# A two-layer streaming encoder on one core: attention cut into stages, a new order at the head, casts and rates moved

## The chip, the cores and the metric

The kernel runs on one core of one Trainium2 chip. A core has TensorE (PE: matrix products into the accumulators' memory, PSUM), VectorE (DVE), ScalarE (ACT), GpSimd (POOL) and SyncE (SP), which work through their own instructions in order and wait for one another through semaphores. DMA transfers are issued from the queues of SP, ACT or POOL. The metric is the device time of one execution in microseconds (us), as the median of several runs.

## The reference

x is 256 tokens by 2048 channels, c one conditioning row. Two layers, all in fp32:

```python
for l in range(DEPTH):
    mod = (c_act @ w_mod[l] + b_mod[l]).reshape(bn, 6, d)
    shift_m, scale_m, gate_m, shift_f, scale_f, gate_f = ...
    h = layer_norm(x) * (1.0 + scale_m) + shift_m
    proj = h @ w_in[l]
    uv, q_c, kv_c, k_r, sb, sc, sh, ag = jnp.split(proj, IN_SPLITS, axis=-1)
    y_a = gmlp_mixer(uv, ...)                 # chunked spatial gating
    y_b = mla_mixer(q_c, kv_c, k_r, ...)      # latent attention, 4 heads
    y_c = short_conv_mixer(sb, sc, sh, ...)   # width 3
    y_d = conformer_conv(ag, ...)             # GLU, width 31, norm, swish
    y = jnp.concatenate([y_a, y_b, y_c, y_d], axis=-1) @ w_out[l]
    x = layer_norm(ALPHA * x + (1.0 + gate_m) * y, ...)
    h = layer_norm(x) * (1.0 + scale_f) + shift_f
    y = conv_ffn(h, ...)                      # 2048 -> 2 x 5632 -> 2048
    x = layer_norm(ALPHA * x + (1.0 + gate_f) * y, ...)
```

The attention normalises q_c and kv_c by their root mean square, makes queries, keys and values from them, rotates a part of the queries and one shared key, and takes a softmax over the keys of the same or earlier 64-token chunks.

## The kernel before

**Weights.** Every weight is read once, in tiles of 1 MB (`raw_tile`, four buffers) or 512 KB. Most are split into two halves of a rounded type, so that a product costs three fast passes: ScalarE casts the high half (`whi`, line 397), DVE subtracts for the low half (`wlo`, line 398). Some tiles are used "exact" (`wexact`, line 381), as plain fp32 without a split; a plain product is issued as two records of TensorE.

**Modulation.** `w_mod` is multiplied by c on DVE, in passes over 1 MB tiles: `row_sum` (line 192) for shifts and scales, `mod_step` (line 227) for gates. A generator, `mod_stream`, deals these passes out. `stream` (line 339) calls `pump` once for each unit of products, and `RATES` (line 35) says how many passes a unit of each stage takes along.

**Scheduling.** The code gives the order of the program. A scheduler then sets the order on each engine: earlier code has precedence, and later instructions that are ready go ahead where an earlier one waits. `tc.add_manual_dep` adds a dependency by hand, one kind for order on the same engine alone, the other with a semaphore.

**Head.** SP's queue begins with the identity matrix (`cst`), the columns of c (`ccol`), x and the first mod weights. ScalarE applies Silu to c; products with a matrix of ones spread it over the partitions (`cB`). `normed_T` takes the statistics of x for two tiles of 128 tokens, each with its own root (`power`, on POOL); ScalarE normalises a quarter, TensorE transposes it, and ScalarE copies it to `hF`.

**Layer 0's mixers**, `by_pieces`, go through the 16 blocks (kt) of 128 channels of h as they come: for each, two mod passes, one `mod_done` (line 205), then the scale and shift on `hF` (line 1455). From block `PLAIN_KT` = 4 on, `hF` is split into `hT` by `split` (line 415: the cast on ScalarE, line 417, the subtraction on DVE, line 418). `turns` lists the order of products: groups D, U, V, B and E, with D's accumulators in PSUM throughout and the others' sums held outside, brought in (line 1224) and put back (line 1229) by ScalarE. The copy that puts back is ordered behind the casts of the D tile, if that is the very next turn. Then B's remaining units run, and `mix_b` at their end; then C's units (`mix_ce`), then the output projection.

**Attention**, `mix_b` (line 958), loads its weights (into three raw buffers in layer 1), reads B's accumulators out (squares, scaled copies), and goes straight on: sums of squares (`ps_ss`), roots, rotated key (`ps_kr`), queries (`ps_qn`, `ps_qr`), keys (`ps_kn`), values (`ps_v`), scores and softmax for three groups (`ps_sc`), transposes (`ps_pT`) and the weighted values (`ps_o`). All of this comes in the program ahead of the first products of group C.

PSUM has six banks for accumulators and two for short-lived tiles (`ms_tile`). `load_params` loads the small parameters of a layer on POOL's queue. Both kinds of background work, the taps of the 31-wide convolution (`prodD` on ScalarE, `convD` on DVE in layer 0), are dealt out by `STEPS`.

## Time and profile before

| What | Value |
|---|---|
| median of 3 runs | 2246.07 us (2244.87 to 2246.17) |
| the profiled execution | 2246.46 us |
| its span, first to last instruction | 2244.7 us |
| mean granted TensorE clock | 0.991 |
| HBM read | 601.05 MB |

The profile gives the busy time of each engine, in total and by windows of time, with the clock granted to TensorE and the share of time in which the 16 DMA engines worked. In a timeline each row is a run of like instructions: start, length, engine, line, operation, tile written <- tiles read, count; in brackets the idle time of the engine ahead of it and what ended it. Records of TensorE overlap slightly.

### The profile page before, as it was taken

Reading aid. Unit: us, or ns where it says so; the run is one execution under the profiler, and the core shown is the slowest. Engines: PE = TensorE matmul, PEld = TensorE weight load, DVE = VectorE, ACT = ScalarE, POOL = GpSimd, SP = SyncE. Lnnn points to the kernel's source line nnn. Section 1 sums busy time; section 2 is a strip of 40 time slices with the busy share of each in tenths; the row PEclk is TensorE's granted clock in tenths of the full one; section 3 lists DMA queues with packets and bytes.
Section 4 is the critical chain, followed back from the end, with each engine's and each line's share of the span. In section 5 each row is a group of like instructions: output and inputs, shape, how many; then the busy total and the mean of one; then the engine's idle time right before and its main releaser. Section 6 shows DMA issues by size and latency. Waiting matters only on the chain.

```text
span 2244.7 us, 30821 instructions
## 1 busy us (share of the span) xinstructions
PE 2200.6 (98%) x12128; PEld 1901.5 (85%) x12128; DVE 1738.9 (77%) x2222; ACT 1067.3 (48%) x1579; POOL 29.6 (1%) x49
## 2 busy tenths in 40 slices
PE   7999999999999999999999999999999999999997
PEld 5788885898888888888889899888888888888886
DVE  6778986988888888989876998977775656575756
ACT  3457541454455445544444435445444544454542
POOL 0000000000000000000000000000000000000000
PEclk9999999999999999999999999999999999999999
DMA  9999689688888888888867666865665555555553
GB/s 390 350 390 386 239 340 359 247 308 315 313 316 308 329 318 320 328 330 322 336 219 263 209 232 252 305 224 208 245 224 192 184 199 179 203 189 188 187 194 144
DMA packets 94235, 605.17 MB, mean 270 GB/s; under 512 B 10660, under 2 KB 10852, under 8 KB 28932
## 3 DMA queue, kind: packets, MB, share of 16 engines
q1 hardware_dynamic: 93752, 602.29, 71.8%
q8 instruction: 95, 1.56, 0.3%
q0 software_dynamic: 336, 0.89, 0.1%
q14 instruction: 52, 0.43, 0.1%
HBM read 601.05 MB, written 2.10 MB: 269 GB/s over the span
## 4 chain that ended last, share of the span: by engine, by line
PE 80%; DVE 4%; DMA 1%; ACT 1%; issue 1%; POOL 0%; DVEq 0%; ACTq 0%; POOLq 0%
PE g_c L94 23%; PE v_c L94 22%; PE d L94 21%; PE o L94 5%; PE C_c L94 2%; PE D_c L94 2%; PE U_c L94 1%; PE B_c L94 1%; PE E_c L94 1%; DVE wlo L398 1%; DMA wraw<-in_w_out_dram 1%; DVE convD L827 1%; PE ps_xT L534 0%; DVE wmod L192 0%; DMA wmod<-in_w_mod_turned_dram 0%
## 5 line engine op out<-in xcount | busy, mean ns | idle before, releaser
L397 ACT CAST whi<-wraw 128x1024 fp32r<-128x1024 f32 (+1 forms) x632 | 647.9, 1045 | 873.2 <-PE g_c L94 208.1
L398 DVE TENSOR_TENSOR wlo<-wraw,whi 128x1024 fp32r<-128x1024 f32 (+1 forms) x632 | 752.9, 1214 | 307.6 <-ACT whi L397 290.0
L94 PE MATMUL d<-whi,a 128*128 128x512 f32 x1344 | 364.1, 389 | 0.0
L94 PE MATMUL v_c<-hT,whi 128*128 128x512 f32 (+1 forms) x1456 | 341.8, 383 | 0.0
L94 PE MATMUL g_c<-hT,whi 128*128 128x512 f32 (+1 forms) x1344 | 313.3, 380 | 0.0
L192 DVE SCALAR_TENSOR_TENSOR wmod<-wmod,cB 128x2048 f32<-128x2048 f32 x126 | 287.4, 2286 | 31.9 <-DMA wmod<-in_w_mod_turned_dram 31.6
L94 PEld LDWEIGHTS v_c<-hT,whi 128*128 128x128 f32 x1456 | 264.5, 189 | 48.2 <-DVE g L1388 0.3
L94 PEld LDWEIGHTS d<-whi,a 128*128 128x128 f32 x1344 | 252.2, 188 | 52.5 <-ACT whi L397 0.2
L94 PEld LDWEIGHTS g_c<-hT,whi 128*128 128x128 f32 x1344 | 243.4, 189 | 43.2
L94 PE MATMUL d<-wlo,a 128*128 128x512 f32 x672 | 209.9, 389 | 0.0
L94 PE MATMUL v_c<-hT,wlo 128*128 128x256 f32 x1400 | 190.2, 283 | 0.0
L94 PEld LDWEIGHTS v_c<-hT,wlo 128*128 128x128 f32 x1400 | 183.1, 191 | 6.5
L94 PE MATMUL g_c<-hT,wlo 128*128 128x256 f32 x1280 | 175.8, 283 | 0.0
L94 PEld LDWEIGHTS g_c<-hT,wlo 128*128 128x128 f32 x1280 | 168.2, 191 | 5.9
L227 DVE SCALAR_TENSOR_TENSOR macc<-wmod,cact,macc 128x2048 f32<-128x2048 f32 x60 | 140.7, 2345 | 17.3 <-DMA wmod<-in_w_mod_gates_dram 17.2
L94 PEld LDWEIGHTS d<-wlo,a 128*128 128x128 f32 x672 | 126.2, 188 | 26.2
L94 PE MATMUL o<-whi,a 128*128 128x512 f32 x384 | 109.7, 395 | 2.4 <-ACT whi L397 2.4
L94 PEld LDWEIGHTS o<-whi,a 128*128 128x128 f32 x384 | 71.8, 188 | 20.1 <-ACT whi L397 4.1
L94 PE MATMUL D_c<-hT,whi 128*128 128x256 f32 x432 | 81.6, 292 | 1.7 <-ACT whi L397 1.7
L1337 DVE SCALAR_TENSOR_TENSOR u<-g,pf,u 128x254 f32<-128x254 f32 (+1 forms) x176 | 73.3, 476 | 0.0
L94 PEld LDWEIGHTS D_c<-hT,whi 128*128 128x128 f32 x432 | 68.8, 197 | 4.4 <-ACT whi L397 2.8
L94 PE MATMUL o<-wlo,a 128*128 128x512 f32 x192 | 63.0, 397 | 0.6 <-DVE wlo L398 0.5
(343 smaller groups left out, 2505.4 us busy)
## 6 DMA issues: line engine op xcount, KB each, us to landing
wraw<-in_ffn_w_up_dram SPq DMA_DIRECT2D x168, 1024.0 KB, 4.9
wmod<-in_w_mod_turned_dram SPq DMA_DIRECT2D x126, 1024.0 KB, 6.3
wraw<-in_ffn_w_down_dram SPq DMA_DIRECT2D x88, 1024.0 KB, 4.8
wmod<-in_w_mod_gates_dram SPq DMA_DIRECT2D x64, 1024.0 KB, 5.0
wraw<-in_w_in_dram SPq DMA_DIRECT2D x27, 1024.0 KB, 5.5
wraw<-in_w_out_dram SPq DMA_DIRECT2D x26, 1024.0 KB, 5.8
wexact<-in_w_in_dram SPq DMA_DIRECT2D x46, 512.0 KB, 9.6
wexact<-in_ffn_w_up_dram SPq DMA_DIRECT2D x16, 512.0 KB, 9.5
```

Of the source, the lines that this page charges most:

```text
L94: pe.matmul(o, lhsT, rhs, start=start, stop=stop, skip_group_check=True)
L192: i = dve.scalar_tensor_tensor(out=raw, in0=raw, scalar=1.0, in1=cB[:, k0 : k0 + n], op0=ALU.mult, op1=ALU.mult, accum_out=total)
L227: i = dve.scalar_tensor_tensor(out=acc, in0=w, scalar=col, in1=acc, op0=ALU.mult, op1=ALU.add)
L397: cast[0] = act.copy(hi[:, :m], r)
L398: i = dve.tensor_tensor(out=lo[:, :m], in0=r, in1=hi[:, :m].bitcast(F32), op=ALU.subtract)
L827: dve.scalar_tensor_tensor(out=yd[:, j, 30 - k :], in0=glu[:, j, : S - 30 + k], scalar=CW(k, j), in1=yd[:, j, 30 - k :], op0=ALU.mult, op1 ...
L1337: dve.scalar_tensor_tensor(out=u[:, sh:], in0=x[:, : S - sh], scalar=col(k, j), in1=u[:, sh:], op0=ALU.mult, op1=ALU.add)
```

## The change

- **Head.** `ccol` and `cst` are loaded from ScalarE's queue, so x is first on SP's. The matrix of ones is a DVE memset. The two variances are put side by side, and one root serves both tiles. The first `row_sum` waits for that root.
- **Idle products.** `warm` multiplies the ones with some tile into a PSUM tile that nothing reads: once on a constant at the start, once on each token tile's first normalised quarter, and once on the first mod weights.
- **Casts.** The high half of `hT` is copied by DVE. The list of casts ahead of which a sum may not be put back holds the cast of D's weights alone, and reaches over the next two turns.
- **Rates.** Layer 0: group C 1.5 to 2.0, output projection 1.53 to 1.17.
- **Attention.** What follows the read-out of B's accumulators is cut into seven steps. `stream` runs one of them behind the products of each of C's units, from the first unit on. The operations are the same.
- **Parameters.** Layer 1's are loaded behind layer 0's last parameter load.

```diff
-    dict(B=1.3, C=1.5, out=1.53, first=1.2, up=0.68, down=0.7),
+    dict(B=1.3, C=2.0, out=1.17, first=1.2, up=0.68, down=0.7),
...
+    ccol = keep.tile([P, 16], F32, name="ccol")
+    act.dma_start(out=ccol, in_=A["c_cols"])
     cst = keep.tile([P, 1024], F32, name="cst")
-    nc.sync.dma_start(out=cst[:, 0:128], in_=consts[:, 0:128])
+    act.dma_start(out=cst[:, 0:128], in_=consts[:, 0:128])
+    cact = keep.tile([P, 16], F32, name="cact")
+    act.activation(out=cact, in_=ccol, func=AF.Silu)
...
+    flat = slot("flat")[:, :512]
+    pool.memset(flat, 1.0)
+    onesR = keep.tile([P, P], F32R, name="onesR")
+    dve.memset(onesR.bitcast(F32), 1.0)
+    ones = onesR.bitcast(F32)
...
+    def warm(x, n):
+        ps = ms_tile("warm")
+        for _ in range(n):
+            mm(ps[:, : x.shape[1]], ones, x, True, True)
+
+    warm(flat, 1)
...
-        row_sum(raw, D, 0, total)
+        i = row_sum(raw, D, 0, total)
+        if root:
+            tc.add_manual_dep(i.ins, root.pop().ins.name, data_dep, reason="the root is not to wait for this pass")
+            warm(raw[:, 0:512], 1)
...
         item = load()
+        begun = bool(staged)
         flush()
+        if begun:
+            staged.pop(0)()
         pending.append(lambda: products(item))
...
+            steps = (
+                (sums,),
+                (queries, keys_scaled),
+                (keys,),
+                (lambda: scores(0, 0), lambda: scores(1, 0)),
+                (lambda: turned(0, 0), lambda: turned(1, 0), lambda: scores(1, 1)),
+                (lambda: turned(1, 1),),
+                (values,),
+            )
+            staged.extend(lambda fs=fs: [f() for f in fs] for fs in steps)
...
-                    casts[k].append(cast[0])
+                    casts[k] = cast[0]
...
-                g1, k1 = turns[n + 1] if n + 1 < len(turns) else ("", ())
-                side(g, kts, casts.get(k1[0], ()) if g1 == "D" else ())
+                side(g, kts, [casts[k[0]] for h, k in turns[n + 1 : n + 3] if h == "D" and k[0] in casts])
...
-            power(r[:, 0:1], r[:, 0:1])
             scale.append(r)
+        rs = smallp.tile([P, 2], F32, tag="rsin", name="rs_in")
+        root[:] = [power(rs, var)]
...
+            if q == 0:
+                warm(xn, 1)
...
             if kt >= PLAIN_KT:
-                casts[kt] = [split([h[:, kt % 2, :] for h in hT[kt // 2][:2]], x)]
+                hi, lo = (h[:, kt % 2, :] for h in hT[kt // 2][:2])
+                dve.tensor_copy(hi, x)
+                dve.tensor_tensor(out=lo, in0=x, in1=hi.bitcast(F32), op=ALU.subtract)
...
-            load_params(l + 1)
+            load_params(l + 1, params[0])
```

More of the change, by code (lines that the diff above doesn't have):

```diff
@@ L110, in encoder_kernel @@
     sinT = cst[:, 768:1024]
-    flat = tmp_tile("flat")
-    pool.memset(flat[:, 0:P], 1.0)
-    pool.memset(flat[:, P : P + 16], 0.0)
-    for j in range(4):
-        pool.memset(flat[:, P + 5 * j : P + 5 * j + 1], 1.0)
-    onesR = keep.tile([P, P + 16], F32R, name="onesR")
-    act.copy(onesR, flat[:, : P + 16])
-    ones = onesR[:, 0:P].bitcast(F32)
+    flat = slot("flat")[:, :512]
[3 more added lines that the diff above has]
+    ones = onesR.bitcast(F32)
     mhalf = keep.tile([P, 4], F32, name="mhalf")
@@ L124, in power @@
     def power(o, i):
-        pool.tensor_tensor(out=o, in0=i, in1=mhalf[:, : i.shape[1]], op=ALU.pow)
+        return pool.tensor_tensor(out=o, in0=i, in1=mhalf[:, : i.shape[1]], op=ALU.pow)
     X = []
@@ L131, in encoder_kernel @@
         X.append(x_t)
-    ccol = keep.tile([P, 16], F32, name="ccol")
-    nc.sync.dma_start(out=ccol, in_=A["c_cols"])
-    cact = keep.tile([P, 16], F32, name="cact")
-    act.activation(out=cact, in_=ccol, func=AF.Silu)
     W = {
@@ L195, in row_sum @@
         held(i, "mod")
+        return i
+    root = []
     def mod_unit(l, m, kt, total):
@@ L1067, in mix_b, with sums @@
-            for blk in range(2):
+            v = {}
+            def sums():
+                ps = ms_tile("ps_ss")
+                for t in range(2):
+                    for j in range(3):
+                        mm(ps[:, t : t + 1], sqs[j][:, t * P : (t + 1) * P], ones[:, 0:1], j == 0, j == 2)
+                    for j in range(2):
+                        mm(ps[:, 2 + t : 3 + t], sqs[3 + j][:, t * P : (t + 1) * P], ones[:, 0:1], j == 0, j == 1)
+                v["rr"] = rr = smallp.tile([P, 8], F32, tag="rr", name="rr")
+                dve.tensor_scalar(
+                    out=rr[:, 0:2], in0=ps[:, 0:2], scalar1=1.0 / Q_LORA, scalar2=RMS_EPS, op0=ALU.mult, op1=ALU.add
+                )
+                dve.tensor_scalar(
+                    out=rr[:, 2:4], in0=ps[:, 2:4], scalar1=1.0 / KV_LORA, scalar2=RMS_EPS, op0=ALU.mult, op1=ALU.add
+                )
+                power(rr[:, 4:8], rr[:, 0:4])
+                dve.tensor_scalar(out=rr[:, 4:6], in0=rr[:, 4:6], scalar1=ATT_SCALE, scalar2=None, op0=ALU.mult)
+                v["dg"] = dg = tmp_tile("dgB")
+                for t in range(2):
+                    dve.tensor_scalar(
+                        out=dg[:, t * P : (t + 1) * P], in0=ident, scalar1=rr[:, 6 + t : 7 + t], scalar2=None, op0=ALU.mult
+                    )
+                v["rope"] = rope = slot("rope").rearrange("p (j s) -> p j s", j=4)
+                ps = ms_tile("ps_kr")
+                mm(ps[:, :S], idup, kc[0:64, 0:S], True, False)
+                mm(ps[:, :S], rotdup, kc[0:64, S : 2 * S], False, True)
+                pool.memset(rope[64:128, 2, :], 0.0)
+                pool.memset(rope[0:64, 3, :], 0.0)
+                act.copy(rope[0:64, 2, :], ps[0:64, :S])
+                act.copy(rope[64:128, 3, :], ps[64:128, :S])
@@ L1119, in mix_b @@
[L1119 to L1127 removed]
+                v[(blk, g)] = pt
@@ new lines, in turned @@
+            def turned(blk, g):
+                pt = v[(blk, g)]
+                if blk == 0:
+                    v["pT0"] = slot("pT0").rearrange("p (h s) -> p h s", h=4)
+                    v["pT1"] = slot("pT1")[:, :512].rearrange("p (h s) -> p h s", h=4)
+                pT0, pT1 = v["pT0"], v["pT1"]
+                ps = ms_tile("ps_pT")
+                for i in range(4):
+                    pe.transpose(ps[:, i * P : (i + 1) * P], pt[:, i * P : (i + 1) * P], ident)
+                if blk == 0:
+                    dve.tensor_copy(pT0[:, :, 0:P], ps.rearrange("p (h s) -> p h s", h=4))
+                else:
+                    p4 = ps.rearrange("p (h k s) -> p h k s", h=2, k=2)
+                    dve.tensor_copy(pT0[:, 2 * g : 2 * g + 2, P : 2 * P], p4[:, :, 0, :])
+                    dve.tensor_copy(pT1[:, 2 * g : 2 * g + 2, :], p4[:, :, 1, :])
@@ new lines, in values @@
+            def values():
+                vv, pT0, pT1 = v["vv"], v["pT0"], v["pT1"]
+                Y["b"] = slot("yb").rearrange("p (j s) -> p j s", j=4)
+                for b in range(2):
+                    ps = ms_tile("ps_o")
+                    for hh in range(2):
+                        h = 2 * b + hh
+                        o = ps[:, hh * S : (hh + 1) * S]
+                        mm(o, vv[:, 0, h * P : (h + 1) * P], pT0[:, h, :], True, False)
+                        mm(o[:, P : 2 * P], vv[:, 1, h * P : (h + 1) * P], pT1[:, h, :], False, True)
+                    act.copy(Y["b"][:, 2 * b : 2 * b + 2, :], ps.rearrange("p (j s) -> p j s", j=2))
@@ L1408, in normed_T @@
         scale = []
+        var = smallp.tile([P, 2], F32, tag="vin", name="v_in")
         for t in range(2):
```

226 lines of the change are left out of this document (94 added, 132 removed).

## Prediction, written before the result was known

> **What bounds the kernel now.** I read the page first, for the engines' shares, then the busy time by windows, to find where TensorE is idle or its clock is down, and last the waits and timelines of those places.
>
> ```profile
> PE 2200.6 (98%) x12128; PEld 1901.5 (85%) x12128; DVE 1738.9 (77%) x2222; ACT 1067.3 (48%) x1579; POOL 29.6 (1%) x49
> ```
>
> TensorE is busy for all but 2244.7 - 2200.6 = 44.1 us of the span, and half of that lies ahead of its first real product. The change adds products and takes none away, so it can win only idle time and time at a lowered clock.
>
> ```profile
> core 0: us, PE busy (x) PEld busy (x) DVE busy (x) ACT busy (x) POOL busy (x), PEclk, DMA share, GB/s
> 19.90:25.30 5.40, 5.40 (x13) 4.32 (x14) 3.90 (x3) 1.62 (x3) 0.00 (x0) 0.50 1.02 413
> 50.00:58.50 8.50, 8.50 (x39) 6.84 (x39) 1.27 (x4) 2.96 (x6) 0.00 (x0) 1.00 0.84 342
> 58.50:76.80 18.30, 18.06 (x103) 15.12 (x102) 16.03 (x20) 10.01 (x18) 0.00 (x0) 1.00 0.80 309
> 76.80:86.80 10.00, 7.11 (x35) 6.83 (x35) 8.75 (x10) 4.38 (x7) 0.00 (x0) 0.66 0.92 300
> 86.80:208.60 121.80, 119.39 (x656) 101.39 (x654) 100.55 (x109) 67.62 (x128) 4.21 (x8) 1.00 1.00 402
> 208.60:220.00 11.40, 8.84 (x36) 7.77 (x36) 10.24 (x16) 11.25 (x32) 1.02 (x1) 0.70 1.01 413
> 220.00:300.00 80.00, 79.60 (x383) 67.68 (x382) 66.70 (x88) 38.79 (x85) 2.68 (x1) 1.00 0.70 258
> 330.00:347.00 17.00, 14.22 (x57) 9.85 (x56) 14.41 (x15) 5.99 (x6) 0.00 (x0) 1.00 1.00 372
> 1297.40:1325.00 27.60, 27.60 (x160) 23.51 (x160) 25.00 (x55) 8.15 (x15) 1.10 (x1) 1.00 0.53 203
> ```
>
> The losses in reach stand in these rows. At half clock 5.4 us of work cost 2.7 too much (first row). At 76.8 there are 2.9 us idle and 0.34 x 10 = 3.4 lost to the clock; at 208.6, 2.6 idle and 0.30 x 11.4 = 3.4; at 330, 2.8 idle. In layer 1's attention (last row) nothing is idle. But from 86.8 to 208.6 the DMA share is 1.00: there the transfers set the pace, and TensorE can arrive earlier only by as much as they do. They lost 0.16 x 8.5 + 0.20 x 18.3 + 0.08 x 10 = 5.8 us between 50 and 86.8.
>
> **The head.** SyncE issues x third; DVE's first row sum shares its time with the root for tile 1.
>
> ```profile
> 0.74 0.40 SPq L104 DMA_DIRECT2D cst<-in_consts_dram  x1
> 1.19 0.42 SPq L134 DMA_DIRECT2D ccol<-in_c_cols_dram  x1
> 1.66 0.42 SPq L1407 DMA_DIRECT2D x<-in_x_dram  x1
> ```
> ```profile
> 10.99 0.56 POOL L125 TENSOR_TENSOR r_in<-r_in,mhalf 128x1 f32<-128x1 f32 x1 [7.71 <-DVE r_in L1417]
> 13.84 2.59 POOL L125 TENSOR_TENSOR r_in<-r_in,mhalf 128x1 f32<-128x1 f32 x1 [2.29 <-DVE r_in L1417]
> ```
> ```profile
> 13.74 2.28 DVE L192 SCALAR_TENSOR_TENSOR wmod<-wmod,cB 128x2048 f32<-128x2048 f32 x1
> ...
> 18.27 0.16 DVE L205 TENSOR_TENSOR mod<-total,bcol 128x2 f32<-128x2 f32 x1
> 19.43 0.41 DVE L1455 TENSOR_SCALAR hF<-hF,mod 128x256 f32<-128x256 f32 x1 [1.00 <-ACT hF L1430]
> ```
> ```profile
> 5.64 6.64 PE L94 MATMUL ps_c<-diag,onesR 128*128 128x512 f32 x8 [5.64 <-DVE diag L160]
> ```
>
> With the two small loads on ScalarE's queue, x is issued at 0.74 and everything behind it on SyncE moves 0.92 us. ScalarE pays two issues of some 0.4 us ahead of the Silu, which waits for its data anyhow. The shared root starts when tile 1's statistics are there, at 13.84 - 0.92 = 12.9, and takes 0.6 (the lone row) instead of 2.59, since the row sum now waits for it. Queued behind that wait on DVE are both sums and the first mod, all needed by the first product: 13.5 + 2 x 2.28 + 0.16 + 0.41 = 18.6, and with the few hundredths between the rows 18.7. ScalarE's path, which ended last before (the 1.00 us wait in the last DVE row), is then done sooner, at about 17. The first product comes at 18.7 for 19.90: 1.2.
>
> The idle products are four pairs of 512-column records. At ps_c's 6.64 / 8 = 0.83 us they take 6.6 at half clock, 3.3 at full. Three pairs stand between the root and 18.7, in time that TensorE has idle, so I cost them at nothing; were the last one late, it would cost up to 1.7. The pair that reads the first mod weights holds their raw buffer by as much, and SyncE's next load waits for it, beside a DMA that is full (1.02). If they hold the clock up, the 2.7 goes; I take 2.0, as the switch comes at an instant that no row fixes. Head: 1.2 + 2.0 = 3.2, between 0.9 (the issue alone) and 3.9.
>
> **The order of the casts.** This is the largest term (layer 0's D group, with the others' turns between its tiles).
>
> ```profile
> 54.99 0.58 ACT L1229 COPY sumU<-U 128x512 f32<-128x512 f32 x1 [6.99 <-PE U L94]
> ...
> 58.20 0.42 ACT L417 CAST hT<-hF 128x256 fp32r<-128x256 f32 x1
> 58.50 1.05 ACT L397 CAST whi<-wraw 128x1024 fp32r<-128x1024 f32 x1
> ```
> ```profile
> 58.65 0.42 DVE L418 TENSOR_TENSOR hT<-hF,hT 128x256 fp32r<-128x256 f32 x1 [7.23 <-ACT hT L417]
> 59.59 1.23 DVE L398 TENSOR_TENSOR wlo<-wraw,whi 128x1024 fp32r<-128x1024 f32 x1 [0.52 <-ACT whi L397]
> ```
> ```profile
> 50.73 0.33 SPq L386 DMA_DIRECT2D wraw<-in_w_in_dram  x1
> 60.84 0.33 SPq L200 DMA_DIRECT2D wmod<-in_w_mod_turned_dram  x1
> ```
>
> A cast of hT stood on ScalarE behind copies that waited for TensorE's U products; DVE waited 7.23 us for it, its raw buffers stayed full, and SyncE issued nothing from 50.73 to 60.84. The new code makes hT's high half on DVE, and puts the casts of D's weights ahead of the sum copies when D is one or two turns away; U(2,3) was not covered before. DVE then gets past at about 52, wlo at 53.5, and the queue refills some 7 us earlier. The added DVE copies are 12 of 128x256: I take 0.41 (the hF row; not shown itself, between nothing and that), 4.9 us in all, against twelve round trips to ScalarE of about the same length that fall away. A sum copy now waits for a cast, and so for a transfer; behind it TensorE's next bank waits, but D's products of that same cast stand ahead of that.
>
> TensorE would win 3.2 + 6.3 by 86.8 if nothing else bound. The transfers win 0.9 + 5.8 = 6.7. Behind 86.8 the smaller one counts: **-6.7 at 208.6** for head and casts together, between 0.9 (the stall only moves) and 9.5.
>
> **Attention, layer 0.**
>
> ```profile
> 206.17 4.75 ACT L848 ACTIVATE prodD<-gluD,pm 128x242 f32<-128x242 f32 x12 [1.41 <-DVE convD L849]
> 210.82 1.43 ACT L978 ACTIVATE sqB<-B_c 128x256 f32<-128x256 f32 x5
> ...
> 214.04 0.83 ACT L982 ACTIVATE qg<-B_c,pm 128x256 f32<-128x256 f32 x2
> ```
> ```profile
> 206.79 1.89 PE L94 MATMUL C_c<-hF,wexact 128*128 128x256 f32 x8
> 211.24 0.65 PE L94 MATMUL ps_ss<-onesR,sqB 128*128 128x1 f32 x4 [2.56 <-ACT sqB L978]
> ```
>
> TensorE stood at ps_ss for squares that ScalarE made late, behind a dozen products of the convolution. Now C's first unit stands ahead of ps_ss. Of its 32 records, 20 need no bank of B (six banks, three with B): 20 x 1.89 / 8 = 4.7 us, to 211.5. The fourth bank wants B's first bank read, which before ended near 214.5. So the gain lies between 0 (TensorE waits 3.0 us there, and the clock falls again) and 6.0 (ScalarE reads the bank in time, as where its order puts the squares ahead of the dozen). The rows favour neither; I take the middle, **-3.0**. The steps themselves keep every instruction, so their TensorE time is the same; what is queued behind each step is the next unit of C, and the softmax of ScalarE and DVE now has such a unit, 32 x 0.236 = 7.6 us, to lie beside.
>
> The Trainium skill, TensorE: Matmul & The Clock Gate, section Part 1, has the clock fall after an idle window of about 3.4 us. The trace disagrees in part: it fell after 2.56 us, beside thin one-column products. By that rule the 3.0 us wait would keep the clock, the low end would be 3.0 and the term 4.5.
>
> **Rates.** C takes 8 x 2.0 instead of 12 mod steps, out's eleven units 12.9 instead of 16.8: four passes move. C's stage has DMA room (0.70 over 80 us). DVE goes from 66.7 to 66.7 + 4 x 2.28 = 75.8 of 80 there: nearly full, and its slack was the cover; I take +1.0 (0 to 3). In out, the first five units, which come ahead of the idle time at 330, ask for 5 x 0.36 = 1.8 passes less; at 1.05 MB each and the 413 GB/s of a full DMA that is 4.6 us, more than the 2.8 idle: **-2.6** (0 to 2.8).
>
> **Attention, layer 1.** TensorE was never idle there; 0, between -1 and the rival below. The parameters' wait for layer 0's last load stands on POOL, with nothing urgent behind it: 0.
>
> **Sum**, against this execution (2244.7 span, 2246.46 run, 0.4 above the median 2246.07): -6.7 - 3.0 + 1.0 - 2.6 = -11.3, so 2246.07 - 11.3 = **2234.8**.
>
> **Rivals.**
>
> *Slower: C waits for its weights in layer 1.*
>
> ```profile
> 1296.14 0.33 SPq L280 DMA_DIRECT2D wmod<-in_w_mod_gates_dram  x1
> 1305.37 0.33 SPq L386 DMA_DIRECT2D wraw<-in_w_in_dram  x1
> ```
> ```profile
> wraw<-in_w_in_dram SPq DMA_DIRECT2D x27, 1024.0 KB, 5.5
> ```
>
> Attention's weights there take three of the four raw buffers, so C's second unit was issued only at 1305.37. Before, the query products filled that time. In stages they stand behind that unit, if the scheduler keeps program order: C's first unit and the sums end near 1305.4, the weights land at 1305.4 + 5.5, the casts take 1.05 + 1.23, so 7.8 idle and 3.4 of clock: 11.2. The third unit's buffer comes free only behind the queries, so it comes twice: 22.4. Then 2234.8 + 22.4 = 2257.2. It decides as soon as C's second products stand ahead of the queries on TensorE; for it, the free buffer; against it, TensorE's order before mixed C freely into attention. Chance 0.12; once only, 2246: 0.08.
>
> *The stall moves.* The first cast waits for its own transfer instead, 0.9 remains of 6.7: 2240.6, near the bound. Speaks for it: D's weights are also late by DMA at 76.8. Chance 0.20.
>
> *All of it works*: attention -6.0, out -2.8, C's passes free: 2246.07 - 6.7 - 6.0 - 2.8 = 2230.6, and down to 2225 where some of the 2.4 idle behind 86.8 goes and head and clock come in full. Chance 0.20.
>
> **How the numbers follow.** The forecast, 2231 to 2239, has 0.40. The range, 2224 to 2248, holds the forecast, the better case, the moved stall and the single wait, and leaves out 0.12 above and some 0.05 below. 0.2%, or 4.5 us, is about what a measurement tells from no change: the line is 2241.6. Faster: 0.40 + 0.20 + half of 0.20 = 0.70. Same: the other 0.10 and the 0.08 = 0.18. Slower: 0.12.
>
> **What would show it.** Right: first D product near 18.7 at a full clock; SyncE without a 10 us hole at 50 to 61; no half clock at 76.8 to 86.8; DVE never idle 7 us for hT; no idle at 330 to 347. Attention: ps_ss behind C's first unit, and whether a C product waits for ScalarE. Wrong: DMA share still under 0.9 between 50 and 80, a half clock near 211, or idle time at C's products near 1300.

## The result, and the profile after

The changed kernel takes **2257.72 us** (median of six runs, 2255.08 to 2262.33), the kernel before 2246.12 in the same comparison (2244.55 to 2247.11). The ratio is 1.0055, with a 95% interval of 1.0042 to 1.0069: slower by about 12 us, where the forecast was 11 us faster. The range ended at 2248, so it doesn't hold the time either.

The profiled execution of the changed kernel took 2262.33 us (span 2260.5). It is the slowest of its six, 4.6 us above their median, and this has to be kept in mind: a part of what its trace shows is not in every run.

The page's row of TensorE comes first, in the layout of the row before.

```profile
PE 2205.6 (98%) x12136; PEld 1902.4 (84%) x12136; DVE 1742.8 (77%) x2235; ACT 1061.0 (47%) x1565; POOL 25.2 (1%) x43
```

TensorE is busy 5.0 us longer, with eight records more (the idle products), and idle for 2260.5 - 2205.6 = 54.9 us instead of 44.1: 10.8 of the 15.8 us that the span grew by are waiting.

I compare the two traces by stages. Each time is the end of the last product of a group, in us from the start of the span.

| end of | before | after | the stage alone |
|---|---|---|---|
| first D product (its start) | 19.90 | 24.21 | +4.3 |
| D, layer 0 | 156.18 | 158.17 | -2.3 |
| B, layer 0 | 206.95 | 213.95 | **+5.0** |
| C, layer 0 | 303.74 | 314.64 | **+3.9** |
| out, layer 0 | 404.40 | 417.37 | +2.1 |
| B, layer 1 | 1297.63 | 1308.61 | -2.0 |
| C, layer 1 | 1372.70 | 1387.73 | **+4.0** |
| the last product | 2232.95 | 2248.77 | +0.8 |

The busy time by windows, for the changed kernel, at the places that answer to those of before:

```profile
core 0: us, PE busy (x) PEld busy (x) DVE busy (x) ACT busy (x) POOL busy (x), PEclk, DMA share, GB/s
24.20:29.60 5.40, 5.40 (x26) 4.75 (x25) 5.33 (x7) 0.23 (x1) 0.00 (x0) 1.00 1.04 426
49.40:63.20 13.80, 11.90 (x65) 10.04 (x63) 2.60 (x6) 4.61 (x9) 0.00 (x0) 1.00 0.47 189
158.20:169.60 11.40, 7.40 (x55) 6.79 (x55) 4.21 (x6) 10.05 (x15) 1.06 (x2) 1.00 1.01 404
213.90:233.00 19.10, 16.24 (x59) 13.43 (x58) 11.35 (x16) 12.12 (x34) 1.01 (x1) 0.68 0.69 282
...
314.60:331.60 17.00, 12.52 (x53) 9.22 (x51) 17.00 (x25) 7.86 (x12) 0.60 (x1) 1.00 0.73 272
1308.60:1336.20 27.60, 26.66 (x163) 24.50 (x162) 23.69 (x56) 6.24 (x10) 1.10 (x1) 0.88 0.33 116
```

The first row is the one success: the first products run at full clock (1.00, before 0.50), though 4.3 us late. The second row is the stretch in which the casts should have kept the transfers going: the DMA share is 0.47, where before has 0.66 over the same time. In the third, a stretch in which before had no loss of its own, 4.0 us are idle. The fourth and the last are the two attentions: clock 0.68 and 0.88. The fifth shows out's first units with DVE busy for all 17.00 us and TensorE idle for 4.5. The same stretch of before, from the end of C's products on, has DVE nearly as busy and TensorE never idle:

```profile
303.74:320.74 17.00, 17.00 (x75) 13.74 (x75) 16.89 (x23) 7.94 (x12) 0.60 (x1) 1.00 0.79 312
```

**The head.** Rows of the timelines of before (the first fence) and of the changed kernel, ScalarE, DVE, GpSimd and TensorE (start and duration in us, then the instruction; in brackets the idle time before it and what ended it):

```profile
3.95 0.22 ACT L136 ACTIVATE cact<-ccol 128x16 f32<-128x16 f32 x1
4.90 2.49 DVE L160 TENSOR_TENSOR diag<-cst,cact 128x512 f32<-128x512 f32 x4
```
```profile
5.96 0.22 ACT L108 ACTIVATE cact<-ccol 128x16 f32<-128x16 f32 x1 [3.03 <-DMA ccol<-in_c_cols_dram]
```
```profile
8.90 2.50 DVE L163 TENSOR_TENSOR diag<-cst,cact 128x512 f32<-128x512 f32 x4 [1.73 <-DMA cst<-in_consts_dram]
```
```profile
17.03 0.72 POOL L126 TENSOR_TENSOR rs_in<-v_in,mhalf 128x2 f32<-128x2 f32 x1 [14.99 <-DVE r_in L1465]
```

Both small loads were issued by 1.2 us, on ScalarE's queue, yet ScalarE waits for the columns of c until 5.96 (before, cact was done by then: it ran at 3.95), and DVE for the identity until 8.90 (before, the same four instructions began at 4.90). They shared the DMA engines with x and the first weights. The trace's packet records show how: the columns of c are 128 packets of 64 bytes, the identity 128 of 512 bytes, and they started 16 at a time, one such group each 0.31 us, the columns from 2.80 to 5.4 us and the identity up to 8.2. A packet of x or of the weights, 8 KB, takes 0.31 us. So between two small packets an engine moved one large one. DVE works in order: x's statistics stand behind that wait, and the root runs at 17.03 instead of the forecast 12.9. The root itself takes 0.72 us, as foreseen.

**The casts.** ScalarE and SyncE's queue, changed kernel:

```profile
58.52 1.07 ACT L1479 COPY hF<-ps_xT 128x512 f32<-128x512 f32 x2 [8.94 <-PE ps_xT L1478]
59.84 1.07 ACT L1479 COPY hF<-ps_xT 128x512 f32<-128x512 f32 x2 [0.26 <-PE ps_xT L1478]
60.82 1.05 ACT L413 CAST whi<-wraw 128x1024 fp32r<-128x1024 f32 x1
```
```profile
49.40 0.33 SPq L402 DMA_DIRECT2D wraw<-in_w_in_dram  x1
63.15 0.33 SPq L209 DMA_DIRECT2D wmod<-in_w_mod_turned_dram  x1
```

The cast of D's first split weights is ahead of the sum copies, as the change says. But four other copies of ScalarE, those of x's transposed quarters to `hF`, stand ahead of it and wait 8.94 us for transposes that TensorE does behind U's products. SyncE issues nothing for 13.7 us (before: 10.1).

**The parameters' wait.** GpSimd, DVE and TensorE, changed kernel:

```profile
153.38 0.54 POOL L188 DMA_DIRECT2D pf<-in_ffn_cols_dram  x1
161.76 0.53 POOL L188 DMA_DIRECT2D bcol<-in_b_mod_cols_dram  x1 [7.85 <-DMA pf<-in_ffn_cols_dram]
```
```profile
167.50 0.18 DVE L149 TENSOR_SCALAR bcol<-bcol 128x32 f32<-128x32 f32 x1 [7.19 <-DMA bcol<-in_b_mod_cols_dram]
167.59 1.22 DVE L414 TENSOR_TENSOR wlo<-wraw,whi 128x1024 fp32r<-128x1024 f32 x1
```
```profile
168.87 0.50 PE L94 MATMUL V<-wlo,hT 128*128 128x512 f32 x1 [4.00 <-DVE wlo L414]
```

Layer 1's parameters now wait for layer 0's last load, on GpSimd, where indeed nothing urgent stands behind. But DVE has an instruction of 0.18 us that adds 1 to them (`scales_up`), and it stands in DVE's order among layer 0's work. DVE idles 7.19 us for it, the low half of V's weights is made behind it, and TensorE waits 4.00 us.

**Attention.** TensorE, changed kernel, layer 0 and then layer 1:

```profile
213.78 4.91 PE L94 MATMUL C_c<-hF,wexact 128*128 128x256 f32 x22
221.56 4.63 PE L94 MATMUL C_c<-hF,wexact 128*128 128x256 f32 x10 [2.86 <-ACT qg L998]
225.99 4.26 PE L94 MATMUL ps_ss<-onesR,sqB 128*128 128x1 f32 x20
```
```profile
1314.21 2.29 PE L94 MATMUL ps_ss<-onesR,sqB 128*128 128x1 f32 x20
1316.43 2.05 PE L94 MATMUL ps_kr<-kc,cst 64*128 64x256 f32 x4
1318.41 0.80 PE L94 MATMUL C_c<-hT,whi 128*128 128x256 f32 x2
```

In layer 0, C's first unit reaches the bank that B still holds and waits 2.86 us; then come all 20 sums of squares in a row. The 20 take 4.26 us here and 2.29 in layer 1: in layer 0 they run at half clock. In layer 1 TensorE is nowhere idle in these rows, and still the products behind the sums take twice as long as ahead of them (0.80 for two of C's, 0.40 before 1314). The granted clock is 0.50 from 1316.5 for 6.8 us.

### The profile page after: what moved, and what is told of

It reads as the page before. It is cut to its first block, busy times and chain, and to the rows that moved or that the text cites. A ratio compares the mean times of both kernels' runs of the same rounds, so it can differ in the third digit from the quotient of the medians.

```text
span 2260.5 us, 30863 instructions
## 1 busy us (share of the span) xinstructions
PE 2205.6 (98%) x12136; PEld 1902.4 (84%) x12136; DVE 1742.8 (77%) x2235; ACT 1061.0 (47%) x1565; POOL 25.2 (1%) x43
## 4 chain that ended last, share of the span: by engine, by line
PE 81%; DVE 3%; DMA 1%; issue 1%; ACT 1%; POOL 0%; DVEq 0%; SPq 0%; POOLq 0%; ACTq 0%
PE g_c L94 22%; PE v_c L94 22%; PE d L94 21%; PE o L94 6%; PE C_c L94 2%; PE D_c L94 2%; PE U_c L94 1%; PE B_c L94 1%; PE E_c L94 1%; DVE wlo L414 1%; DVE convD L843 1%; DMA wraw<-in_w_out_dram 0%; PE ps_xT L550 0%; DVE wmod L198 0%; PE ps_gate L94 0%
```

## The experiments

Three questions: which part of the change costs the 12 us; why the casts brought nothing; and what takes the clock down in attention. All ratios are to the kernel before, on the same chip.

| kernel | made from | median us | ratio, 95% interval |
|---|---|---|---|
| e1_params | after | 2251.59 | 1.0029 [1.0018, 1.0040] |
| e2_small | after | 2248.45 | 1.0016 [1.0006, 1.0026] |
| e3_inline | after | 2258.47 | 1.0055 [1.0042, 1.0069] |
| e5_wide | after | 2254.41 | 1.0041 [1.0028, 1.0054] |
| f1_two | e1 + e2 | 2247.98 | 1.0011 [1.0002, 1.0020] |
| f2_two_wide | f1 + e5 | 2246.74 | 1.0006 [0.9997, 1.0015] |
| f3_rates | f2, old rates | 2246.88 | 1.0009 [1.0000, 1.0017] |
| f4_nowarm | f2, no idle products | 2249.20 | 1.0021 [1.0012, 1.0030] |
| g1_late | f1, layer 1's addition late | 2245.41 | 1.0002 [0.9993, 1.0011] |
| g2_late_wide | g1 + e5 | 2241.37 | 0.9989 [0.9980, 0.9998] |
| g3_banks | g2, B's banks read in turn | 2240.86 | 0.9981 [0.9972, 0.9990] |
| h1_casts | before + casts | 2246.51 | 1.0012 [1.0003, 1.0020] |
| k1_order | h1, ScalarE's order | 2240.64 | 0.9980 [0.9971, 0.9988] |
| k2_after_order | after, ScalarE's order | 2251.40 | 1.0033 [1.0020, 1.0045] |
| k3_order_wide | k1 + e5 | 2239.24 | **0.9972 [0.9961, 0.9983]** |

### One part at a time, from the changed kernel

**e1_params**: layer 1's parameters are loaded without the wait.

```diff
-            load_params(l + 1, params[0])
+            load_params(l + 1)
```

> The changed kernel with layer 1's parameters loaded without the wait. Theory (DVE stands behind scales_up, which waits for a parameter load that the new wait and a full DMA make late): DVE's 7.2 us idle at 160 and TensorE's 4.0 us at 165 are gone, B's products end 4 to 6 us earlier against the end of D, and the time falls by 4 to 6 us, to about 2252.5. Rival (the DMA sets the pace of that stage, and the wait only shows where the lack of weights would have stood): the idle time moves to another instruction and the time stays within 1.5 us of the changed kernel's.

The ratio falls from 1.0055 to 1.0029, that is by 0.0026 x 2246 = 5.8 us. B ends 50.7 us behind D (after: 55.8, before: 50.8), and TensorE's gap at V is 0.42 instead of 4.00. So the wait costs what the trace showed, as was expected. But the same short addition of DVE now stands in the head, as it did in before (timeline of DVE, e1_params):

```profile
8.01 0.18 DVE L149 TENSOR_SCALAR bcol<-bcol 128x32 f32<-128x32 f32 x1 [0.72 <-DMA bcol<-in_b_mod_cols_dram]
9.71 2.50 DVE L163 TENSOR_TENSOR diag<-cst,cact 128x512 f32<-128x512 f32 x4 [1.52 <-DMA cst<-in_consts_dram]
```

The first D product comes at 24.57 (after: 24.21). In this run the addition itself delays nothing, for the identity comes later still, and ends the last wait of DVE at 9.71. With the small loads first this changes, as f1 below shows: so the wait that the change added had a use, since it took that addition out of the head. It only put it at a worse place.

**e2_small**: the two small loads go first on SyncE, ahead of x.

```diff
-    act.dma_start(out=ccol, in_=A["c_cols"])
+    nc.sync.dma_start(out=ccol, in_=A["c_cols"])
...
-    act.dma_start(out=cst[:, 0:128], in_=consts[:, 0:128])
+    nc.sync.dma_start(out=cst[:, 0:128], in_=consts[:, 0:128])
```

> The changed kernel with the two small loads back at the head of SyncE's queue, ahead of x. Theory (behind x and the mod weights on the shared DMA engines the small loads land late, and DVE, which needs them first, holds up the statistics): identity lands before 5, cB is complete before 13.5, the first product of D comes at 18 to 20 instead of 24.2, and the time falls by 2 to 4 us, since D's stage gave back half of the delay. Rival (the shared root and the idle products are what is late): the first product stays behind 22.

The ratio falls to 1.0016: 8.8 us, where 2 to 4 were expected. TensorE's timeline of the head, and DVE's:

```profile
18.71 1.91 PE L94 MATMUL warm<-xn,onesR 128*128 128x512 f32 x2
20.41 1.23 PE L94 MATMUL warm<-wmod,onesR 128*128 128x512 f32 x2
21.48 3.62 PE L94 MATMUL D_c<-hF,wexact 128*128 128x256 f32 x16
```
```profile
19.57 0.41 DVE L1506 TENSOR_SCALAR hF<-hF,mod 128x256 f32<-128x256 f32 x1 [0.86 <-ACT hF L1479]
```

The first product starts at 21.48, 2.7 us sooner than after, and its input is ready at 19.57 + 0.41 = 19.98: the last idle products, which stand ahead of it on TensorE, hold it for 1.5 us. It is still later than before (19.90), but its 16 records take 3.62 us instead of 6.35. More than the head changed, though. D ends at 150.81, 7.4 us ahead of after, and the 13.7 us hole of SyncE is gone: in this kernel the scheduler put the four copies of x behind the cast. That made the cause of the 8.8 us ambiguous, and it is why k1 and k2 were run.

**e3_inline**: attention goes straight on, in the order of before, with all else as changed.

```diff
-            steps = (
...
-            staged.extend(lambda fs=fs: [f() for f in fs] for fs in steps)
+            sums()
+            keys_scaled()
+            queries()
+            keys()
+            for blk, g in ((0, 0), (1, 0), (1, 1)):
+                scores(blk, g)
+                turned(blk, g)
+            values()
```

> The changed kernel with the attention run at once, in the order of before. Theory (the staging costs the clock in both layers, as all sums of squares then stand in one row): no half clock behind ps_ss in layer 1, group C there takes 75 instead of 79 us, layer 0's C stage 97 instead of 101, and the time falls by 4 to 8 us. Rival (C's stages are slower by the four more mod passes in layer 0 and by the late DVE): only layer 1 gains, or neither, 0 to 3 us.

2258.47 and the same ratio to the fourth place. Without stages, the wait in layer 0 is again at the sums of squares (2.57 us), the clock still falls there (10.2 us long) and in layer 1 (6.8). The 4 to 8 us expected did not come: the staging by itself neither won nor lost anything that can be measured.

**e5_wide**: each sum of squares is a product of 128 equal columns instead of one, and the root reads the first of each. Each sum then stands in 128 equal columns.

```diff
-    mm(ps[:, t : t + 1], sqs[j][:, t * P : (t + 1) * P], ones[:, 0:1], j == 0, j == 2)
+    mm(ps[:, t * P : (t + 1) * P], sqs[j][:, t * P : (t + 1) * P], ones, j == 0, j == 2)
...
-    out=rr[:, 0:2], in0=ps[:, 0:2],
+    out=rr[:, 0:2], in0=ps.rearrange("p (a b) -> p a b", b=P)[:, 0:2, 0],
```

> The changed kernel with the sums of squares made as products of 128 columns instead of one, equal in number; the results are the same. Theory (a row of one-column products counts as idle for the clock): each record keeps its 0.1 us, since the weights' load sets it, no half clock follows in layer 1 (6.8 us at half before, so 3.4 us), and less of the 13.7 us at half in layer 0; the time falls by 3 to 6 us. Rival (the clock falls for the idle time of TensorE alone): both spells of half clock stay, and the time is the same.

1.0041 against 1.0055, 3.1 us; the two intervals overlap. Its windows, for the same two stretches behind B's end, and TensorE's timeline in layer 0:

```profile
212.60:231.70 19.10, 16.23 (x84) 13.88 (x83) 16.79 (x21) 18.63 (x50) 1.89 (x1) 1.00 0.73 289
1300.20:1327.80 27.60, 26.37 (x183) 24.32 (x182) 26.57 (x61) 6.36 (x10) 1.09 (x1) 1.00 0.35 127
```
```profile
220.24 2.42 PE L94 MATMUL C_c<-hF,wexact 128*128 128x256 f32 x10 [2.87 <-ACT qg L998]
222.50 2.39 PE L94 MATMUL ps_ss<-onesR,sqB 128*128 128x128 f32 x20
```

The wait of 2.87 us is still there and the clock is 1.00 all the same; the 20 wide products take 2.39 us, the thin ones 2.29. By itself this one profile would not carry much; why this wait kept the clock is told in the last section. Over the profiles of all kernels of this study and the two they start from: behind the wait in layer 0, the ten with thin sums show 3.4 to 13.7 us at half clock (8.2 on the mean), the seven with wide sums 0 or 3.4. In layer 1, where TensorE doesn't wait ahead of the sums, the clock fell right behind them in five of the ten with thin sums and in none of the seven with wide ones (two of these show 3.4 us at half clock some 16 us later, behind a wait of TensorE). So thin sums don't bring the clock down each time, but it is they that do it in layer 1 (the last section says when); in layer 0 the wait does it too, and the thin products make the spell longer on the mean. In time the wide sums win little: in the four pairs of runs that differ by them alone (the changed kernel and e5, f1 and f2, g1 and g2, k1 and k3) the ratio falls by 0.0005 to 0.0014, and the intervals overlap each time.

### Together

**f1_two** is e1 and e2 in one; **f2_two_wide** adds e5; **f3_rates** is f2 with the rates of before; **f4_nowarm** is f2 without the idle products.

```diff
-    dict(B=1.3, C=2.0, out=1.17, first=1.2, up=0.68, down=0.7),
+    dict(B=1.3, C=1.5, out=1.53, first=1.2, up=0.68, down=0.7),
```
```diff
-        for _ in range(n):
+        for _ in range(0):
             mm(ps[:, : x.shape[1]], ones, x, True, True)
```

The first of these diffs is f3's, the second f4's, each against f2.

> The changed kernel with both repairs, the parameters' wait and the small loads. Theory (the two losses are separate, 5.9 and 8.8 us by the runs above): 2257.7 - 14.7 = 2243.0 on the scale of the first runs, or 2 us under the kernel before, ratio 0.999. Rival (they overlap, as an earlier D stage only waits longer for V's low halves): no better than the small loads alone, ratio 1.001 to 1.002.

> Both repairs and the sums of squares as products of 128 columns. Theory (thin products lower the clock, in both layers): 3 to 5 us under the kernel with both repairs, ratio 0.997, with no half clock between 200 and 230 or between 1290 and 1320. Rival (the clock falls by the phase of its windows, and the run with wide sums had luck): within 1.5 us of it, and half clocks at other places.

> The kernel of the run above with the old rates (1.5 in C, 1.53 in the output projection). Theory (DVE reaches the output projection with mod passes still to do, and its first products wait 3.2 us for low halves): the 3.2 us gap falls under 1, and the time falls by 1 to 3 us. Rival, as forecast (four passes fewer relieve the full DMA of the output projection): the old gaps of 2.8 us come back there, and the time rises by up to 3 us.

> Both repairs and wide sums, without the idle products. Theory (they hold the clock up, for 2.7 us, and are themselves 1.5 us late): first product of D near 20.0 instead of 21.5, at half clock, D's first 16 records 6.3 instead of 3.6 us, and the time 1 us more or the same. Rival (the transfers set the pace from there on, and nothing of the head counts): the same within 0.5 us, with D's end the same.

f1 did not add up: e1's 5.8 and e2's 8.8 make 14.6, but f1 is only 9.9 below the changed kernel (1.0011). DVE's timeline of f1 says why:

```profile
8.81 0.18 DVE L149 TENSOR_SCALAR bcol<-bcol 128x32 f32<-128x32 f32 x1 [2.83 <-DMA bcol<-in_b_mod_cols_dram]
8.90 2.49 DVE L163 TENSOR_TENSOR diag<-cst,cact 128x512 f32<-128x512 f32 x4
```

The identity has long landed now, but layer 1's addition stands ahead of it on DVE and waits for its own load. The first product is at 24.61 again.

f2 is 0.0005 below f1, 1.1 us and inside the intervals; the 3 to 5 us expected did not come. The half clock behind the sums in layer 1 is gone, but others stand at 211.4, in the wait of 2.87 us ahead of C's fourth bank, and at 1320.7, behind a wait of 2.65 us of C for a cast of its weights, and a rotated query waits 2.25 us in layer 0, where f1 has none over 0.4.

f3 says what the rates do, term by term. From B's end to C's end the old rates take 96.0 us and the new ones 98.0 (f3 and f2); from there to the end of out, 99.8 and 103.0. So the new rates cost 1.9 and 3.2 us there. Then f3 waits 5.63 us for the norm behind out, and f2 2.81, and f3's clock spell there is 6.8 us long against 3.4: 2.8 + 1.7 come back. The times differ by 0.0003, within their intervals. Rates: nothing, neither the 1 to 3 us less that were expected nor the rival's 3 us more.

f4 does not tell what it was meant to. The time rises by 0.0015, 3.4 us, and the first D products run at a clock of 0.66 instead of 1.00, but the four copies of x stand ahead of the cast again in this kernel, so that D ends at 158.3 (f2: 153.5). What the idle products are worth by themselves in time stays open. What they do to the clock shows over all profiles: in each of the twelve with idle products D's first 3 us run at full clock, in each of the five without (before, f4, h1, k1, k3) at half.

### Mended, and the casts alone

**g1_late** is f1 with DVE's addition for layer 1 ordered behind the last block of h. **g2_late_wide** adds the wide sums. In **g3_banks**, ScalarE then reads B's first bank completely (two squares, two scaled copies) before it goes to the next, so that C's fourth bank comes free sooner. **h1_casts** is the kernel before with the change of the casts and nothing else: `hT`'s high half on DVE, and the sum copies behind the casts of D one or two turns away.

```diff
-            load_params(l + 1, params[0])
+            load_params(l + 1)
...
-            scales_up(l)
+            tc.add_manual_dep(scales_up(l).ins, last_x[0].ins.name, order_dep, reason="not ahead of the head")
```
```diff
-            for i in range(5):
-                ps, o = bank[i]
...
+            square(0)
+            square(1)
+            scaled(0)
+            scaled(1)
+            square(2)
+            square(3)
+            scaled(2)
+            square(4)
```

In the texts on record for g2 and g3, "the kernel before" is the run listed just before, g1 and g2.

> The changed kernel with the small loads first on SyncE, layer 1's parameters loaded without a wait, and DVE's addition on them ordered behind the last block of h. Theory (both runs that dropped the wait only moved DVE's stall from 160 to the head, where it stood behind the same load ahead of the products with c; with neither stall the two gains add): first product near 21.5, no DVE wait of over 2 us for a parameter load, D's end near 151, B's end near 201, ratio 0.998 to 0.999. Rival (the DMA sets the pace up to B's end, so that V's low halves are late anyhow): B's end stays at 204 or later, ratio 1.001.

> The kernel before with the sums of squares as products of 128 columns. Theory (thin products lower the clock): no half clock within 15 us behind the sums in either layer, 2 to 4 us less, ratio 0.997. Rival (the clock falls by the phase of its windows): half clocks elsewhere and the same time.

> The kernel before with ScalarE reading B's accumulators bank by bank, so that the first is free after four reads instead of seven and four products of the convolution. Theory (C's fourth bank waits for B's first): TensorE's gap of 2.9 us at C's first unit falls under 1, the time by 2 to 4 us, ratio 0.996. Rival (ScalarE comes to the squares too late whatever their order): the gap stays over 2 us and the time is the same.

> The kernel before with the change of the casts alone (high half of h on DVE, D's weight casts ahead of the sum copies over two turns). Theory, the prediction's largest term: D's end comes 5 to 7 us before 156.2, the half clock at 80 goes, SyncE's hole of 10 us at 50 to 61 shrinks, and the time falls by 4 to 7 us, ratio 0.997 to 0.998. Rival (the stall moves to the weights' own transfer, as the hole of 13.7 us in the changed kernel says): D's end within 2 us of 156, ratio 1.000.

g1 is level with before (1.0002): the whole 12 us are back. Three things differ from the changed kernel by intent: small loads first, no wait for the parameters, and no DVE instruction of layer 1 in the way. But a fourth came along, for in g1, as in e2 and f1, the scheduler put the copies of x behind the cast. D ends at 149.3, B at 200.2, 6.7 us ahead of before, as expected; behind that the clock is 0.69 over C's first 19 us, and by the end of out in layer 0 only 0.9 us of the lead are left, so the ratio expected, 0.998 to 0.999, was missed. With the wide sums (g2) it is 0.9989, for 0.997 expected, and the clock still falls in C's wait, for 3.4 us. g3 cuts C's wait from 2.87 to 0.96 us, but 1.66 us come up at the queries, beside a wait of 2.20 at the rotated ones that g2 has too (2.25); 0.9981, not to be told from g2, for 0.996 expected.

h1 is the surprise: the largest term of the forecast, alone, gains nothing (1.0012). Its rows, ScalarE and SyncE:

```profile
56.20 1.07 ACT L1429 COPY hF<-ps_xT 128x512 f32<-128x512 f32 x2 [8.93 <-PE ps_xT L1428]
57.53 1.07 ACT L1429 COPY hF<-ps_xT 128x512 f32<-128x512 f32 x2 [0.26 <-PE ps_xT L1428]
58.50 1.05 ACT L397 CAST whi<-wraw 128x1024 fp32r<-128x1024 f32 x1
```
```profile
50.55 0.33 SPq L386 DMA_DIRECT2D wraw<-in_w_in_dram  x1
60.83 0.33 SPq L200 DMA_DIRECT2D wmod<-in_w_mod_turned_dram  x1
```

The same four copies, a wait like that of the changed kernel (8.93 us for 8.94), and the same hole as before. D ends at 155.92, before at 156.18.

### The order on ScalarE

Two causes were possible for the casts' failure: those copies, or that transfers set the end of D whatever happens at 50. **k1_order** is h1, and **k2_after_order** the changed kernel, with one order added: the copies of x's third quarter come behind the cast of D's first split weights. **k3_order_wide** is k1 with the wide sums.

```diff
-            act.copy(hF[q][:, :, t * P : (t + 1) * P], ps.rearrange("p (j t) -> p j t", j=4))
+            i = act.copy(hF[q][:, :, t * P : (t + 1) * P], ps.rearrange("p (j t) -> p j t", j=4))
+            if q > 1:
+                tc.add_manual_dep(i.ins, casts[4].ins.name, order_dep, reason="the first split block is waited for")
```

> The kernel before with the change of the casts alone, and ScalarE's copies of x's third quarter to hF (two instructions, one for each token tile) ordered behind the cast of D's first split weights; nothing else. Theory (the order on ScalarE is what ate the gain): without this order four of these copies stood ahead of the cast and waited 8.9 us for transposes, which stand on TensorE behind U's products; SyncE issued nothing from 50.6 to 60.8. With it the cast runs near 50.6, DVE gets past near 52, SyncE's hole falls to about 3 us, the 1.6 us gap of TensorE at 58 goes, and D ends near 151, 5 us ahead of 155.9; of these, attention's clock and its waits let 3 to 5 through: near 2242, ratio 0.998. Rival (transfers from 60 to 208 set the end of D whatever happens at 50, the 5 us of the run with the small loads first came from the head): the hole goes, D ends at 155 to 156, and the time is 2246, ratio 1.000 to 1.001.

> The changed kernel with the same order of ScalarE's copies of x's third quarter behind the cast of D's first split weights; nothing else. Theory: the stall at 60 goes (PE gap 1.6 at 60.3 and SyncE's hole 49.4 to 63.2), D ends near 153 instead of 158.2; the parameters' wait behind it stays (gap near 4 at 160): 2252 to 2254, 4 to 6 below the changed kernel, ratio 1.003. Rival (transfers set the end of D): D ends at 158, 2257, ratio 1.005.

> The kernel before with the change of the casts, the order of ScalarE's copies, and the sums of squares of attention as products of 128 equal columns instead of one (the root reads the first of each); attention at once, the head and the rates as before. Theory: the gain of the casts (about 4) and the clock at 213 in layer 0 (half for 6.8 us, 3.4 lost) add up: 2238 to 2240, ratio 0.997; layer 1 gains nothing, as its clock did not fall. Rival (the clock at 213 falls by the 2.6 us wait itself, not by the thin products): as the run without the wide sums, 2242.

ScalarE, SyncE and windows of k1:

```profile
50.55 1.05 ACT L397 CAST whi<-wraw 128x1024 fp32r<-128x1024 f32 x1 [3.19 <-DMA wraw<-in_w_in_dram]
54.35 0.59 ACT L1229 COPY sumU<-U 128x512 f32<-128x512 f32 x1 [2.75 <-PE U L94]
...
57.66 1.07 ACT L1429 COPY hF<-ps_xT 128x512 f32<-128x512 f32 x2
```
```profile
50.33 0.33 SPq L386 DMA_DIRECT2D wraw<-in_w_in_dram  x1
52.97 2.73 SPq L200 DMA_DIRECT2D wmod<-in_w_mod_turned_dram  x2
```
```profile
50.30:63.70 13.40, 13.40 (x70) 10.67 (x69) 8.33 (x14) 7.56 (x12) 0.00 (x0) 1.00 1.02 416
86.80:168.60 81.80, 79.42 (x457) 66.26 (x457) 67.39 (x84) 40.72 (x64) 3.33 (x6) 1.00 1.00 398
```

The cast runs 8 us sooner, as soon as its weights land; SyncE's hole is 2.6 us (a pause of 7.1 us follows at 57.9, which the transfers under way cover: the DMA share in it is 1.02); the DMA share from 50 to 64 is 1.02 and TensorE isn't idle there. D ends at 151.16, 5.0 ahead of before, and the time is 0.9980 of before: 4.5 us. From h1 to k1 only this order differs, and the intervals lie apart: 0.0032, 7.2 us, of which 4.8 stand at D's end. The attentions hold some of the rest, for h1's profile has half clock there for 13.7 us in all and k1's for 6.8. k2 gains 1.0055 - 1.0033 = 0.0022, 4.9 us, over the changed kernel, and its D ends at 152.78 (158.17). The theory of the order holds; that of the transfers as a bound whatever happens at 50 falls.

k3 is 0.9972, the fastest of all and faster than both kernels. Over k1 that is 0.0008, within the intervals. Its clock still falls behind the wait in layer 0 (2.57 us, ahead of the first wide sum), for 3.4 us instead of 6.8. So the wait alone can take it down. Waits of 2.87 us with wide sums did so in f2, f3, f4 and g2 too; e5's did not.

## Why the prediction was wrong

A reading at its start was off, though no term hangs on it: of the 44.1 us that TensorE was idle, not half but 19.90 - 8.42 = 11.5 us lie ahead of the first D product, and another 11.8 behind the last product.

**The casts, -5.8 of the term of -6.7: the size was right, the order was missed.** The prediction followed the instructions that the diff moves, sums and casts, and said "DVE then gets past at about 52, wlo at 53.5". k1 shows just that (wlo at 51.72 to 52.94), with 5.0 us at D's end for the 5.8. What failed is the step "the new code ... puts the casts of D's weights ahead of the sum copies", taken as if the cast were then first: with the sum copies out of the way, the scheduler had put the copies of x ahead of it, and these wait for TensorE behind U just like the sum copies did. A row of it stood in the trace of before, between the sum copies and the cast:

```profile
57.20 0.59 ACT L1430 COPY hF<-ps_xT 128x512 f32<-128x512 f32 x1
```

The rival "the stall moves" had the outcome, and another mechanism (the cast waiting for its own transfer). That transfers set the pace behind 86.8 was right: in k1 the DMA share is 1.00 there, and what D won, it won by the transfers. DVE's added copies took 0.29 us each, inside the bounds given for them.

**The head, -0.9: wrong in sign.** The failing step is "ScalarE pays two issues of some 0.4 us ahead of the Silu, which waits for its data anyhow". It took the small loads to land as they did before, when they were first in line; now each of their packets waited for a large one. ScalarE had its columns 2.0 us later, DVE its identity 4.0, and DVE, in order, took the statistics along. With the small loads first (e2), the chain on DVE came as worked out: the root's start 13.24 for 12.9, the first mod at 18.55. ScalarE's path did not come "at about 17" but at 19.5, since transposes and copies stood behind idle products on TensorE, and the last idle products were late by 1.5, inside the 1.7 that the prediction kept for it. The clock came as said, and more: 6.35 - 3.62 = 2.7 us for 2.0, the whole of what the prediction put at stake.

**The parameters' wait, 0: it costs 5.8.** "With nothing urgent behind it" was true of GpSimd's queue and asked of the wrong engine. The question was who reads the data: a 0.18 us instruction in the middle of DVE's order. This is the largest error that comes from a row not looked for.

**Attention in layer 0, -3.0: nothing, the low end.** C's fourth bank wants B's first, as the prediction said, and TensorE waits 2.86 us for the 3.0 it gave, behind 22 of C's records for 20; ScalarE did not read the bank in time. The low end of 0 was still too kind to the profiled run, where the clock spell became 13.7 us instead of 6.8. e3 says that stages or none is the same. The page TensorE: Matmul & The Clock Gate of the Trainium skill, section Part 1, has the clock fall after an idle window of about 3.4 us, counted from no fixed point. By that rule a wait of under 3 us keeps the clock; e5 with 2.87 us agrees, k3 with 2.57 and f2, f3, f4 and g2 with 2.87 do not. What decided in these runs is where the wait fell (last section).

**Attention in layer 1, 0: +1 to +4.** No wait of C for its weights appeared, so the slower rival is not what happened: the longest gap of TensorE in that stage is 0.94 us, at a rotated query. That gap stays in e1, k2 and g1, whose stage is 76 us for 75 before. (A wait of C for the cast or the low half of its weights, of 0.4 to 2.7 us, does appear in e5, f2, f3, f4, g2 and g3, all with wide sums: the rival's place at a fraction of its price.) In the profiled run 6.8 us at half clock, 3.4 lost, come on top. The forecast looked for idle time only, and the clock fell with none.

**Rates, +1.0 and -2.6: +1.9 and +3.2, and back at the norm.** Two steps failed. One is "four passes move": from B's end to C's end DVE begins 17 passes with the new rates and 16 with the old, so one moves (it is busy there for 81.0 us, 80.3 before, for the 9.1 more that were forecast). The other is that transfers end last in out's first units. With the change, DVE does, at a DMA share of 0.73: the two passes just ahead of C's end, C's end work and then single passes stand ahead of the casts' low halves. It is their order that counts and not how busy DVE is, since before had 16.89 us of 17.00 there and no wait of TensorE.

**The sum.** By the ratios the parameters cost 5.8; by the profiles the head costs 1.6 (with the casts at work in both, D ends at 152.78 in k2 and at 151.16 in k1, though k2's first product is 4.1 us later); the casts gave 0 for -5.8; attention and rates gave 0 or above. The rest of the 12.4, some 5 us by difference, is clock and short waits in the attentions and in out. A second pair says much the same: g1, where head, parameters and casts are in order, ends D 1.9 us ahead of k1 and takes 0.0022, 4.9 us, longer, so what the change does behind D costs some 6.8. Beyond what e3 (staging) and f3 (rates) say, no experiment splits this further, and it differs from run to run.

## What to carry to other kernels

When a load or a wait is moved, ask which engine reads the data and what stands behind that reader in its order; the queue that issues it is only half of the question. When one instruction is moved out of another's way, list everything the engine has between the two, not only what the diff names, for in these kernels the scheduler filled the place with the next instruction, and that waited for the same thing. And a row of very thin products is a risk for TensorE's clock even where TensorE never stops; making them 128 columns wide cost 0.1 us here. A small load of 128 short rows was 128 packets here: put it ahead of the large ones on their queue, and not beside them on another.

## What the runs showed of the hardware

- All half-clock spells inside the kernels are 3.4, 6.8, 10.2 or 13.7 us long: one, two, three or four times 3.4. In each of the 17 profiles all switches of the granted clock lie on one grid of 3.413 us, to within 0.01 us. Where a wait falls on this grid decides. A grid line cuts e5's wait of 2.87 us into 1.28 and 1.58, and the clock stays; f2's, as long, lies with 2.66 us in one interval, and the next runs at half clock (windows of e5, two intervals, then of f2, the interval of the wait and the next):

```profile
215.24:218.65 3.41, 2.13 (x10) 1.52 (x9) 3.41 (x4) 3.41 (x12) 0.00 (x0) 1.00 1.01 408
218.66:222.07 3.41, 1.83 (x9) 1.63 (x10) 3.05 (x5) 3.41 (x11) 0.00 (x0) 1.00 1.01 420
```
```profile
207.97:211.38 3.41, 0.75 (x4) 0.32 (x2) 3.39 (x6) 3.41 (x11) 0.00 (x0) 1.00 1.01 408
211.38:214.79 3.41, 3.20 (x8) 2.57 (x9) 2.85 (x4) 3.41 (x10) 0.00 (x0) 0.50 1.02 422
```

- Over all profiles, from 20 us on: each of the 36 full-clock intervals in which TensorE was idle for more than 2.0 us was followed by half clock, of the 46 with 1.5 to 2.0 us ten were, and of over 10,000 with less, none (intervals with sums of squares left aside in the last two counts).
- The granted clock fell behind 20 products of one column (2.29 us) and no idle time, as at 1316.5 in the changed kernel. It did so in all nine intervals of the grid that hold the row of 20 (to within 0.3 us), in none of the five that hold 12 to 17 of them and no idle time, and in none of the seven that hold a row of 20 products of 128 columns. That is why, of the ten kernels with thin sums, only five lost the clock in layer 1.
- A load of 8 KB, issued first of all on ScalarE's queue beside 2 MB of x on SyncE's, was waited for until 5.96 us. Issued on SyncE ahead of x, it was there by 2.4 (e2). The 64 KB of the identity: 8.9 against 3.2. The page DMA: Bandwidth & Descriptors of the Trainium skill, section Queues, rings and completion order, says that each DMA engine serves its queues in turn, packet by packet. The trace agrees: 128 packets of 64 bytes came in 8 groups of 16, one each 0.31 us, the time of one 8 KB packet, and 8 x 0.31 = 2.5 us. So this load's delay was set by the number of its packets and by the size of those that it took turns with.
